# Fifteen weight tiles split afresh in every block instead of stored and read back, and splits pinned in ScalarE's order

## The chip, the cores and the metric

One core of a Trainium2 chip runs the kernel. The metric is device time in microseconds (us) of one execution. The kernel before took 2684.38 us, the median of three runs from 2678.17 to 2687.7 us.

## The reference

One inference step of a hybrid recurrent layer, all in fp32: 2048 prompt tokens and 8 x 8 sample tokens of width 1024 go through two branches (a gated linear recurrence, "LRU", and a gated delta rule with 8 heads, "GDN"), which are merged by sigmoid gates and projected.

```
u = rms_norm(x, norm_pre)                                  # [tokens, 1024]
z = u @ w_in                                               # 1024 x 8208
lru_x, lru_gate, q|k|v, gdn_gate, b, a, m_lru, m_gdn = split(z)
lru_out = rg_lru(conv4(lru_x)) * silu(lru_gate)
gdn_out = gated_delta(silu(conv4(q|k|v)), b, a) * silu(gdn_gate)
merged  = sigmoid(m_lru) * (lru_out @ w_br_lru) + sigmoid(m_gdn) * (gdn_out @ w_br_gdn)
x_new   = x + rms_norm(merged @ w_out, norm_post)
```

The columns m_lru and m_gdn of w_in are the merge gates: 16 tiles of 128 columns.

## The kernel before, in words

The prompt is worked in four blocks of 512 tokens; the 64 sample tokens ride along in block 0, so that a projection there has 576 columns, in two matmul widths of 256 and 320, and 512 columns in blocks 1 to 3. A block runs through stages: the input is normalised and transposed into eight tiles `u` (`u_norm`, `u_tile`); then the K stage (for each of 8 heads a K tile with its convolution, then a merge-gate tile), the LRU stage (8 LRU tiles, 7 more merge-gate tiles between them, 4 gate tiles), the GDN stage (Q, V and gate tile of each head, and the delta rule woven between their matmuls), the branch projections, and the output projection, into which the next block's `u` transposes are woven.

A fp32 product is made of three matmuls: a weight tile W is split into hi (rounded to the matmul's fp32r type) and lo = W - hi, the activations likewise, and a projection tile runs hi x hi, hi x lo, lo x hi for each of 8 slices of 128 rows, 24 matmuls for each width (L551, L553, L555). There are 88 weight tiles. In block 0 each is loaded raw, split (`split`: ScalarE writes hi, L143; GpSimd writes lo, L205; VectorE for the last 8), used, and stored to DRAM with both halves, 1 MB, as `dW`; in blocks 1 to 3 all 88 are read back from `dW`. `worder` lists the tiles in order of use, `wfetch` gets the next ones, `wload` issues a raw load, `wstore` the stores. In block 0 the split tiles live in a ring of three buffers `whl` and `wfetch` runs one tile ahead of the projection; later `whx` is a fourth buffer and it runs three ahead. A new split may write a buffer only when TensorE is done with the tile in it and, in block 0, when that tile's store has landed.

TensorE's order is written by the program: `Weave` decides when the other stages' generators run between a projection's matmuls. The other engines' orders, and that of the DMA issues on SyncE's queue (SP), are set by a scheduler when the program is built; every engine then runs its list strictly in order. Before, `A.after = wlast[0]` (L544) makes every ScalarE operation traced after a projection's start follow the newest weight split: the split may be placed early, but nothing newer before it. Projections write three PSUM banks (`pmm`); ScalarE or VectorE must empty a bank before TensorE can use it again. In the K stage ScalarE copies a K tile out (`cvr`, `cvy`, `cvs`), VectorE convolves it (L582, L588), ScalarE makes the tanh of it (`th`), VectorE the product `kT` (L597), TensorE the head's Gram matrix (`g<-kT`); of the merge-gate tile ScalarE makes `tmo`, at once from PSUM. `er` is the head's decay matrix: a DMA, GpSimd (L756, L757), ScalarE.

Of the kernel before, what the change touches and what calls it, by code (L numbers as in the profile page):

```python
# [22 lines left out]
F32 = mybir.dt.float32  # L23
# [42 lines left out]
LM = 7  # L66
# [88 lines left out]
def body(ctx, tc, x_prompt, x_sample, state_lru_conv, state_lru_h, state_gdn_conv, state_gdn_S,  # L155
# [84 lines left out]
    wstores, wraws = [], {}  # L240

    wready = []
    wlast = [None]
    wnext, lnext = [0], [0]
    ring, wx = [0], []

    def wtile():
        ring[0] += 1
        if wx and ring[0] % 4 == 0:
            return wx[0].tile([128, 2, 1024], F32R, name="whx", tag="whx")  # L250
        return wp.tile([128, 2, 1024], F32R, name="whl", tag="whl", bufs=3)

    def wload(n):

        src, c = e = worder[n]
        if key(e) in wraws:
            return
        if isinstance(c, tuple):
            raw = rw.tile([128, 4, 256], F32, name="rawo", tag="raws")
            SP.dma_start(raw, src[c[1] * 512:(c[1] + 1) * 512, c[0] * 256:(c[0] + 1) * 256]  # L260
                         .rearrange("(k p) c -> p k c", p=128))
            wraws[key(e)] = raw
        elif not (paired[0] <= n < paired[1] or paired[2] <= n < paired[3]):
            raw = rw.tile([128, 8, 128], F32, name="raws", tag="raws")
            SP.dma_start(raw, src[:, c:c + 128].rearrange("(k p) c -> p k c", p=128))
            wraws[key(e)] = raw
        else:
            two = [key(x) for x in worder[n:n + 7]].count((src.tensor.name, c + 128))
            w = 128 + 128 * two
            raw = rp[0].tile([128, 8, w], F32, name="raw", tag="raw")  # L270
            SP.dma_start(raw, src[:, c:c + w].rearrange("(k p) c -> p k c", p=128))
            for j in range(1 + two):
                wraws[src.tensor.name, c + 128 * j] = raw[:, :, 128 * j:128 * j + 128]
# [7 lines left out]
    def wfetch(ahead):  # L281

        while wnext[0] < len(worder) and len(wready) < ahead:
            n = wnext[0]
            e = worder[n]
            place = wplace[key(e)]
            out = isinstance(e[1], tuple)
            hl = wtile()
            hi, lo = (hl[:, j].rearrange("p (k c) -> p k c", c=256 if out else 128) for j in range(2))
            if n < len(wplace):  # L290
                while lnext[0] < len(wplace) and lnext[0] <= n + (
                        2 if paired[0] <= lnext[0] < paired[1] else 1):
                    wload(lnext[0])
                    lnext[0] += 1
                wstore(1)
                wlast[0] = split(hi, lo, wraws[key(e)], V if out else None)
                wstores.append((place, hl))
            else:
                wstore()
                SP.dma_start(hl.bitcast(F32), dW[place])  # L300
            wready.append((hi, lo))
            wnext[0] += 1
# [44 lines left out]
    def u_tile(xh, k):  # L347
        hi = pA.tile([128, TB + NS], F32R, name="a", tag="a")
        lo = pA.tile([128, TB + NS], F32R, name="a", tag="a")
        for gi, grp in enumerate([xh[:4]] + ([xh[4:]] if len(xh) > 4 else [])):  # L350
            t = gtile()
            n = 0
            for xt, m in grp:
                tr(t[:, n:n + m], xt[:m, k * 128:(k + 1) * 128], ident[:m, :m])
# [57 lines left out]
    with tc.tile_pool(name="init", bufs=2, side="right") as ip:  # L412
        with tc.tile_pool(name="u0", bufs=1) as up:
            r0 = ip.tile([8, 128], F32, name="r0")
            SP.dma_start(r0, rows(norm_pre))
            xh = u_load(0, up)
            t = gtile()
            tr(t[:, :8], r0, ident[:8, :8])
            V.tensor_copy(npre, t[:, :8])
            wraw = ip.tile([128, 8, 16], F32, name="wraw", bufs=1)  # L420
            SP.dma_start(wraw, win[:, C_B:C_B + 16].rearrange("(k p) c -> p k c", p=128))
# [8 lines left out]
            V.memset(zz, 0.0)  # L430
            V.tensor_copy(wst[:, 256:352], zz)
            V.tensor_copy(wst3[:, :, 0:16], wraw)
# [98 lines left out]
    for blkno in range(NBLK):  # L531
        if blkno == 1:
            rw_cm.__exit__(None, None, None)
            wx.append(ctx.enter_context(tc.tile_pool(name="wx", bufs=1, side="right")))
            ring[0] = 0
# [5 lines left out]
        def proj(mov, evac):  # L541
            w = nextw()
            wfetch(3 if blkno else 1)
            A.after = wlast[0]  # L544
# [808 lines left out]
```

## Time and profile before

| | |
|---|---|
| runs | 2687.7, 2678.17, 2684.38 us; median 2684.38 |
| profiled execution | 2683.59 us, span 2681.9 us |
| busy share: TensorE, VectorE, ScalarE, GpSimd | 96%, 56%, 33%, 21% |
| mean granted TensorE clock | 0.987 of full |
| DMA | 581.82 MB, mean 217 GB/s |
| blocks 0 to 3 by the stages' starts | 0 to 895, 895 to 1495, 1495 to 2094, 2094 to 2682 us |

Names in the profile are those of the program's tiles, without numbers. PE is TensorE, PEld its weight loads, DVE VectorE, ACT ScalarE, POOL GpSimd, SPq SyncE's queue of DMA issues. L143 is the helper through which all ScalarE activations are issued and L205 the subtraction in `split`, so those groups are told apart by tile: `whl<-raw` on ACT writes a hi half, `whl<-raw` on POOL a lo half. A number in brackets is how long the engine sat idle before an instruction, with what ended that wait.

### The profile page before, as it was taken

The page shows a single profiled execution, that of the slowest core. Times are in us where ns is not written, and L with a number is a line of the kernel's source. Part 1 is how long each engine was busy: PE and PEld are TensorE (multiplying, and loading weights), DVE is VectorE, ACT ScalarE, POOL GpSimd, SP SyncE. Part 2 cuts the span into 40 slices and gives each one's busy share as a digit, 9 for nine tenths or more (in the row PEclk, how much of TensorE's full clock was granted, in tenths as well). Part 3 has the DMA queues.
Part 4 walks back from the last instruction along what each step waited for, and adds up shares of the span by engine and source line. Part 5 has one row for each costly group of instructions (what it writes and reads, how often), then busy time and mean ns, then how long its engine had stood idle before and what let it go on. Part 6 is the DMA issues. An engine that isn't in the chain of part 4 may idle for free.

```text
span 2681.9 us, 39950 instructions
## 1 busy us (share of the span) xinstructions
PE 2571.7 (96%) x15332; PEld 2237.5 (83%) x15332; DVE 1503.4 (56%) x3441; ACT 885.4 (33%) x1722; POOL 565.8 (21%) x444
## 2 busy tenths in 40 slices
PE   6888799999999999999999999999999999999999
PEld 5887798888999788888889888888889888888888
DVE  4668477787434557566522557566513458566512
ACT  5324543333324225333302235333303235333301
POOL 2442342232540211100120121110210211110200
PEclk9988899999999999999999999999999999999999
DMA  7987978789887887554466787544466887555465
GB/s 190 250 257 187 228 207 187 203 176 179 255 292 256 283 277 222 200 177 158 154 237 256 260 283 225 203 163 163 154 245 256 270 272 217 200 172 168 160 236 200
DMA packets 327897, 581.82 MB, mean 217 GB/s; under 512 B 70849, under 2 KB 236762, under 8 KB 282650
## 3 DMA queue, kind: packets, MB, share of 16 engines
q1 hardware_dynamic: 313882, 553.57, 66.9%
q10 hardware_dynamic: 13824, 25.70, 2.5%
q8 instruction: 121, 1.98, 0.3%
q14 instruction: 70, 0.57, 0.1%
HBM read 421.61 MB, written 157.59 MB: 216 GB/s over the span
## 4 chain that ended last, share of the span: by engine, by line
PE 68%; DMA 3%; issue 2%; DVE 1%; POOL 1%; ACT 1%; SPq 0%; ACTq 0%; POOLq 0%; DVEq 0%
PE mm L555 17%; PE mm L551 16%; PE mm L553 16%; PE g L192 5%; PE c L192 4%; PE mm L1294 2%; PE mm L1298 2%; PE mm L1296 2%; PE g L196 2%; DMA er<-dgc 1%; DMA dgc<-gr 0%; DMA npb<-in_norm_post_dram 0%; DMA ux<-in_x_prompt_dram 0%; DMA whl<-dW 0%; POOL er L756 0%
## 5 line engine op out<-in xcount | busy, mean ns | idle before, releaser
L551 PE MATMUL mm<-a,whl 128*128 128x512 f32 (+2 forms) x2432 | 865.0, 356 | 25.2 <-ACT tmo L143 18.5
L555 PE MATMUL mm<-a,whl 128*128 128x512 f32 (+2 forms) x2432 | 869.6, 358 | 4.8 <-POOL whl L205 4.8
L553 PE MATMUL mm<-a,whl 128*128 128x512 f32 (+2 forms) x2432 | 863.9, 355 | 0.0
L551 PEld LDWEIGHTS mm<-a,whl 128*128 128x128 f32 x2432 | 466.7, 192 | 74.7 <-ACT tmo L143 20.0
L555 PEld LDWEIGHTS mm<-a,whl 128*128 128x128 f32 x2432 | 466.7, 192 | 58.0 <-POOL whl L205 5.4
L553 PEld LDWEIGHTS mm<-a,whl 128*128 128x128 f32 x2432 | 466.7, 192 | 45.6
L582 DVE SCALAR_TENSOR_TENSOR cvy<-cvr,cwg,cvy 128x512 f32<-128x512 f32 x288 | 224.7, 780 | 17.8 <-ACT cvy L143 12.4
L553 PE MATMUL mm<-a,whx 128*128 128x512 f32 x448 | 181.7, 406 | 0.0
L555 PE MATMUL mm<-a,whx 128*128 128x512 f32 x448 | 181.4, 405 | 0.0
L551 PE MATMUL mm<-a,whx 128*128 128x512 f32 x448 | 179.3, 400 | 0.0
L1232 DVE SCALAR_TENSOR_TENSOR pt<-tm,mm 128x512 f32<-128x512 f32 (+1 forms) x80 | 47.4, 592 | 189.8 <-PE mm L555 189.8
L143 ACT ACTIVATE cvr<-mm 128x512 f32<-128x512 f32 (+1 forms) x160 | 81.7, 510 | 175.4 <-PE mm L555 167.3
L1086 POOL TENSOR_TENSOR st<-st,mhalf 128x4 f32<-128x4 f32 x32 | 32.3, 1009 | 507.8 <-DVE st L1084 496.0
L205 POOL TENSOR_TENSOR whl<-raw,whl 128x1024 fp32r<-128x1024 f32 x44 | 108.8, 2474 | 118.4 <-ACT whl L143 108.6
L205 POOL TENSOR_TENSOR whl<-raws,whl 128x1024 fp32r<-128x1024 f32 x36 | 89.8, 2495 | 188.6 <-ACT whl L143 176.5
L1296 PE MATMUL mm<-whl,bt 128*128 128x256 f32 x448 | 126.4, 282 | 0.8 <-DVE whl L205 0.8
L1294 PE MATMUL mm<-whl,bt 128*128 128x256 f32 x448 | 126.2, 282 | 0.8 <-DVE y L1303 0.8
L1298 PE MATMUL mm<-whl,bt 128*128 128x256 f32 x448 | 126.2, 282 | 0.6 <-DVE yss L1272 0.6
L143 ACT ACTIVATE th<-cvy 128x512 f32<-128x512 f32 (+1 forms) x96 | 61.9, 644 | 195.7 <-DVE cvy L582 128.6
L143 ACT ACTIVATE yv<-c 128x128 f32<-128x128 f32 x128 | 35.5, 278 | 243.7 <-PE c L192 243.2
L555 PE MATMUL mm<-gp,whl 128*128 128x512 f32 (+2 forms) x296 | 104.2, 352 | 0.0
L551 PE MATMUL mm<-gp,whl 128*128 128x512 f32 (+2 forms) x296 | 104.1, 352 | 0.0
(341 smaller groups left out, 4637.8 us busy)
## 6 DMA issues: line engine op xcount, KB each, us to landing
whl<-dW SPq DMA_DIRECT2D x199, 1024.0 KB
dW<-whl SPq DMA_DIRECT2D x88, 1024.0 KB
whx<-dW SPq DMA_DIRECT2D x65, 1024.0 KB
raws<-in_w_in_dram SPq DMA_DIRECT2D x33, 512.0 KB
raw<-in_w_in_dram SPq DMA_DIRECT2D x15, 1024.0 KB
dtm<-tmo ACTq DMA_DIRECT2D x48, 256.0 KB
tm<-dtm SPq DMA_DIRECT2D x48, 256.0 KB
ux<-in_x_prompt_dram SPq DMA_DIRECT2D x16, 512.0 KB
```

The lines of the kernel that those rows point to most:

```text
L143: r = f(*args, **kw)
L192: T.matmul(out, a, b, start=start, stop=stop)
L196: T.transpose(out, in_, idn)
L205: (eng or G).tensor_tensor(out=lo, in0=src, in1=hi.bitcast(F32), op=OP.subtract)
L551: T.matmul(ps[:, :n], wh, mh[:, c0:c0 + n], start=k == 0, stop=False)
L553: T.matmul(ps[:, :n], wh, ml[:, c0:c0 + n], start=False, stop=False)
L555: T.matmul(ps[:, :n], lo[:, k, :], mh[:, c0:c0 + n], start=False, stop=k == 7)
L582: V.scalar_tensor_tensor(out=y[:, :TB], in0=raw[:, i:i + TB], scalar=cw[:, i, ti:ti + 1], in1=y[:, :TB], op0=OP.mult, op1=OP.add)
L1232: proj(mov, lambda ps, c0, n: V.scalar_tensor_tensor(out=t_[:, c0:c0 + n], in0=x[:, c0:c0 + n], scalar=1.0, in1=ps[:, :n], op0=OP.add, op1 ...
L1294: T.matmul(ps[:, :256], mh[:, cs], wh[:, k % 4], start=k == 0, stop=False)
L1296: T.matmul(ps[:, :256], mh[:, cs], wl[:, k % 4], start=False, stop=False)
L1298: T.matmul(ps[:, :256], ml[:, cs], wh[:, k % 4], start=False, stop=k == 7)
```

## The change

1. Fifteen merge-gate tiles (`whole`) are not stored in block 0. In blocks 1 to 3 they are loaded raw from w_in again, two at a time (a 1 MB pair in one new buffer `wmr`; the last one alone), and split on ScalarE and GpSimd again. `wfetch` issues the next pair's load when a tile of it is at most three ahead and none is held.
2. `A.after` is gone. In block 0 each split is pinned behind the ScalarE operation traced just before it (`tc.keep_in_program_order`). The splits of blocks 1 to 3 are not pinned.
3. The rows of w_in are dealt to partitions eight neighbours at a time (`krows`), for all raw loads of w_in. To match, `u_tile` transposes every eighth column of the input instead of 128 neighbours, so the operand that TensorE loads as weights has a step of 8 elements, 32 bytes; and `norm_pre` is loaded straight into `npre`, without a transpose.
4. Two VectorE operations of the beta/alpha weights (`zz`, the cast of `wraw` into `wst`) are pinned behind older VectorE work.

```
+    NW, NP1 = len(wplace), paired[1]
+    whole = {key(e) for e in mcol[:8 + LM]}
+    def krows(a, by8):
+        return a.rearrange("(p k) c -> p k c", k=8) if by8 else a.rearrange("(k p) c -> p k c", p=128)
...
-                wlast[0] = split(hi, lo, wraws[key(e)], V if out else None)
-                wstores.append((place, hl))
+                tc.keep_in_program_order(split(hi, lo, wraws[key(e)], V if out else None))
+                if key(e) not in whole:
+                    wstores.append((place, hl))
+            elif key(e) in whole:
+                wstore()
+                wload(n)
+                split(hi, lo, wraws.pop(key(e)))
             else:
                 wstore()
                 SP.dma_start(hl.bitcast(F32), dW[place])
+            if wx:
+                for j in range(n + 1, min(n + 4, len(worder))):
+                    if key(worder[j]) in whole:
+                        if not any(x in wraws for x in whole):
+                            wload(j)
+                        break
...
-                tr(t[:, n:n + m], xt[:m, k * 128:(k + 1) * 128], ident[:m, :m])
+                tr(t[:, n:n + m], xt[:m].rearrange("t (p k) -> t k p", k=8)[:, k], ident[:m, :m])
...
-            r0 = ip.tile([8, 128], F32, name="r0")
-            SP.dma_start(r0, rows(norm_pre))
+            SP.dma_start(npre, norm_pre.rearrange("o (p k) -> (o p) k", k=8))
...
-            V.tensor_copy(wst3[:, :, 0:16], wraw)
+            tc.keep_in_program_order(V.tensor_copy(wst3[:, :, 0:16], wraw))
...
-            A.after = wlast[0]
```

TensorE's list is the same in both programs but for the one `npre` transpose that is left out. ScalarE's list at the start of block 0, where `a<-g,npre` empties the transposed input into `u` and `whl<-raws` are the first weight splits, before:

```order
L143 ACTIVATE ux_216<-ux_216,urr 128x1024
L143 ACTIVATE whl<-raws 128x1024
L143 ACTIVATE a<-g,npre 128x512
L143 ACTIVATE a<-g,npre 128x64
L143 ACTIVATE a<-g,npre 128x512
L143 ACTIVATE whl<-raws 128x1024
L143 ACTIVATE a<-g,npre 128x64
```

and now, at the end of the same sixteen copies:

```order
L143 ACTIVATE a<-g,npre 128x512
L143 ACTIVATE a<-g,npre 128x64
L143 ACTIVATE whl<-raws 128x1024 x2
L143 ACTIVATE negA<-negA 128x8
L143 ACTIVATE zr<-mm 32x256
```

Three splits stood between the copies of `u`; now two stand behind all of them, and the third comes a tile later. ScalarE's list at one head in the middle of block 0's K stage, before:

```order
L143 ACTIVATE cvr<-mm 128x256
L143 ACTIVATE cvy<-mm,cwg 128x256
L143 ACTIVATE cvr<-mm 128x256
L143 ACTIVATE cvy<-mm,cwg 128x320
L143 ACTIVATE cvs<-mm 128x8x8
L143 ACTIVATE whl<-raw 128x1024
L143 ACTIVATE th<-cvy 128x576
L143 ACTIVATE tmo<-mm 128x256
```

and now:

```order
L143 ACTIVATE cvr<-mm 128x256
L143 ACTIVATE cvy<-mm,cwg 128x256
L143 ACTIVATE cvr<-mm 128x256
L143 ACTIVATE cvy<-mm,cwg 128x320
L143 ACTIVATE cvs<-mm 128x8x8
L143 ACTIVATE th<-cvy 128x576
L143 ACTIVATE whl<-raw 128x1024
L143 ACTIVATE tmo<-mm 128x256
```

The split has moved behind `th`, which waits for VectorE's convolution, and it is that of one tile earlier in the order of use than the split that stood there. ScalarE's list at the start of block 1's K stage, before:

```order
L143 ACTIVATE cvr<-mm 128x512
L143 ACTIVATE cvy<-mm,cwg 128x512
L143 ACTIVATE th<-cvy 128x512
L143 ACTIVATE tmo<-mm 128x512
L143 DMA dtm<-tmo 128x512
L143 ACTIVATE er<-er 128x512
```

and now, where `whl<-wmr` is the split of a merge-gate tile from its raw pair:

```order
L143 ACTIVATE cvr<-mm 128x512
L143 ACTIVATE cvy<-mm,cwg 128x512
L143 ACTIVATE th<-cvy 128x512
L143 ACTIVATE tmo<-mm 128x512
L143 ACTIVATE whl<-wmr 128x1024
L143 DMA dtm<-tmo 128x512
L143 ACTIVATE er<-er 128x512
```

One split has come in behind each merge-gate tile's `tmo`, in each of blocks 1 to 3.

## Rows read from the trace of the kernel before

**Rows 1.** The page's busy times, and the granted clock in 40 slices.

```profile
PE 2571.7 (96%) x15332; PEld 2237.5 (83%) x15332; DVE 1503.4 (56%) x3441; ACT 885.4 (33%) x1722; POOL 565.8 (21%) x444
PEclk9988899999999999999999999999999999999999
```

**Rows 2.** Busy time by stretch: window, PE, PEld, DVE, ACT, POOL, PEclk, DMA share, GB/s.

```profile
0.00:45.00 45.00, 19.76 (x86) 14.13 (x87) 14.84 (x53) 21.63 (x44) 12.58 (x21) 1.00 0.67 144
52.00:198.00 146.00, 124.69 (x863) 120.46 (x861) 93.34 (x250) 47.12 (x99) 67.75 (x48) 0.93 0.88 255
198.00:345.00 147.00, 119.29 (x801) 116.97 (x800) 102.39 (x253) 78.10 (x140) 47.26 (x29) 0.88 0.85 208
895.00:1495.00 600.00, 597.22 (x3243) 500.79 (x3242) 321.48 (x722) 187.02 (x356) 87.76 (x83) 1.00 0.64 217
```

**Rows 3.** Waits in the start, 0 to 45 us: us in total, times, longest.

```profile
PE g L196 <- DVE a L358: 10.9, 5, 5.9
ACT whl L143 <- DMA raws<-in_w_in_dram: 9.6, 3, 5.5
```

**Rows 4.** Waits in block 0's K stage, 52 to 198 us.

```profile
ACT whl L143 <- DMA dW<-whl: 29.0, 6, 8.8
PE mm L551 <- ACT tmo L143: 14.2, 4, 7.3
PE mm L555 <- POOL whl L205: 2.9, 1, 2.9
```

**Rows 5.** Waits in block 0's LRU stage, 198 to 345 us.

```profile
ACT whl L143 <- DMA dW<-whl: 18.4, 4, 8.1
ACT whl L143 <- issue: 7.0, 1, 7.0
PE g L192 <- ACT lt L143: 15.1, 2, 10.1
```

**Rows 6.** Timeline of the start: start us, us, engine, instruction, count, idle before.

```profile
31.44 1.06 ACT L143 ACTIVATE whl<-raws 128x1024 fp32r<-128x1024 f32 x1 [5.51 <-DMA raws<-in_w_in_dram]
33.92 2.75 PE L196 MATMUL g<-ident,ux 64*128 64x64 f32 x10 [5.94 <-DVE a L358]
```

**Rows 7.** Timeline of block 0, first matmuls of two tiles in a row.

```profile
51.69 0.28 PE L551 MATMUL mm<-a,whl 128*128 128x256 f32 x1
58.09 0.28 PE L551 MATMUL mm<-a,whl 128*128 128x256 f32 x1
```

**Rows 8.** Timeline of block 0's K stage, first head, fourth, and end.

```profile
52.58 0.23 ACT L143 ACTIVATE cvs<-mm 128x64 f32<-128x64 f32 x1
...
110.24 0.23 ACT L143 ACTIVATE cvs<-mm 128x64 f32<-128x64 f32 x1
...
111.50 2.77 POOL L205 TENSOR_TENSOR whl<-raw,whl 128x1024 fp32r<-128x1024 f32 x1 [2.50 <-ACT whl L143]
...
115.29 0.69 ACT L143 ACTIVATE th<-cvy 128x576 f32<-128x576 f32 x1 [3.87 <-issue]
115.88 0.69 ACT L143 ACTIVATE tmo<-mm 128x256 f32<-128x256 f32 x2
...
121.71 0.23 ACT L143 ACTIVATE cvs<-mm 128x64 f32<-128x64 f32 x1
...
124.24 0.28 DVE L588 SCALAR_TENSOR_TENSOR cvy<-cvs,cwg,cvy 128x64 f32<-128x64 f32 x1
...
198.62 0.23 ACT L143 ACTIVATE cvs<-mm 128x64 f32<-128x64 f32 x1
```

**Rows 9.** The transposes into `u`: four in a row in block 0's output projection, and all.

```profile
824.39 0.46 PEld L196 LDWEIGHTS g<-ident,ux 128*128 128x128 f32 x4
...
L196 PE MATMUL g<-ident,ux x136: 270/273/476, 7.7 to 2052.0; 128*128 128x128 f32 x128, 64*128 64x64 f32 x8
```

**Rows 10.** Timeline of block 1's K stage, one head.

```profile
962.62 0.69 DVE L597 SCALAR_TENSOR_TENSOR kT<-th,cvy 128x512 f32<-128x512 f32 x1 [0.50 <-ACT th L143]
...
963.72 1.09 PEld L192 LDWEIGHTS g<-kT 128*128 128x128 f32 x8
```

More of the change, by code (lines that the diff above doesn't have):

```diff
@@ L240, in body, with wtile @@
     wstores, wraws = [], {}
+    NW, NP1 = len(wplace), paired[1]
+    whole = {key(e) for e in mcol[:8 + LM]}
+    def krows(a, by8):
+        return a.rearrange("(p k) c -> p k c", k=8) if by8 else a.rearrange("(k p) c -> p k c", p=128)
     wready = []
-    wlast = [None]
     wnext, lnext = [0], [0]
[L245 to L249, printed above, removed]
+    wx = []
+    def wtile(n):
+        if wx and n % 4 == 0:
             return wx[0].tile([128, 2, 1024], F32R, name="whx", tag="whx")
@@ L262, in wload @@
             wraws[key(e)] = raw
-        elif not (paired[0] <= n < paired[1] or paired[2] <= n < paired[3]):
+        elif not wx and not (paired[0] <= n < paired[1] or paired[2] <= n < paired[3]):
             raw = rw.tile([128, 8, 128], F32, name="raws", tag="raws")
-            SP.dma_start(raw, src[:, c:c + 128].rearrange("(k p) c -> p k c", p=128))
+            SP.dma_start(raw, krows(src[:, c:c + 128], src is win))
             wraws[key(e)] = raw
@@ L269, in wload @@
             w = 128 + 128 * two
-            raw = rp[0].tile([128, 8, w], F32, name="raw", tag="raw")
-            SP.dma_start(raw, src[:, c:c + w].rearrange("(k p) c -> p k c", p=128))
+            raw = (wx[0].tile([128, 8, w], F32, name="wmr", tag="wmr") if wx else
+                   rp[0].tile([128, 8, w], F32, name="raw", tag="raw"))
+            SP.dma_start(raw, krows(src[:, c:c + w], src is win))
             for j in range(1 + two):
@@ L287, in wfetch @@
             out = isinstance(e[1], tuple)
-            hl = wtile()
+            hl = wtile(n)
             hi, lo = (hl[:, j].rearrange("p (k c) -> p k c", c=256 if out else 128) for j in range(2))
@@ L413, in body @@
         with tc.tile_pool(name="u0", bufs=1) as up:
-            r0 = ip.tile([8, 128], F32, name="r0")
-            SP.dma_start(r0, rows(norm_pre))
+            SP.dma_start(npre, norm_pre.rearrange("o (p k) -> (o p) k", k=8))
             xh = u_load(0, up)
-            t = gtile()
-            tr(t[:, :8], r0, ident[:8, :8])
-            V.tensor_copy(npre, t[:, :8])
             wraw = ip.tile([128, 8, 16], F32, name="wraw", bufs=1)
-            SP.dma_start(wraw, win[:, C_B:C_B + 16].rearrange("(k p) c -> p k c", p=128))
+            SP.dma_start(wraw, krows(win[:, C_B:C_B + 16], True))
             u_norm(xh, up)
@@ L429, in body @@
             zz = ip.tile([128, 96], F32, name="zz", bufs=1)
-            V.memset(zz, 0.0)
+            tc.keep_in_program_order(V.memset(zz, 0.0))
             V.tensor_copy(wst[:, 256:352], zz)
-            V.tensor_copy(wst3[:, :, 0:16], wraw)
+            tc.keep_in_program_order(V.tensor_copy(wst3[:, :, 0:16], wraw))
             V.tensor_tensor(out=wst3[:, :, 16:32], in0=wraw, in1=wst3[:, :, 0:16].bitcast(F32), op=OP.subtract)
@@ L534, in body @@
             wx.append(ctx.enter_context(tc.tile_pool(name="wx", bufs=1, side="right")))
-            ring[0] = 0
+            wraws.clear()
         sb = blkno == SB
```

## The prediction

> **What bounds the kernel now.** I read the page first, then busy time by stretch, then the waits of TensorE and ScalarE in the stretches that have gaps, and last the timelines around those gaps. On the page the reader is to see that TensorE is the busy engine, 2571.7 of 2681.9 us, and that its clock falls only in the first seventh of the run [rows 1]. The stretches say the same more sharply: block 1 is busy 597.22 of 600 us at full clock, so there is next to nothing to win in blocks 1 to 3 and something to lose; block 0 is where time lies open [rows 2]. In its K stage TensorE is idle 146 - 124.69 = 21.3 us and runs at 0.93, which costs another 0.07 x 124.69 = 8.7; in its LRU stage it is idle 27.7 and loses 0.12 x 119.29 = 14.3 to the clock; in the first 45 us it is idle 25.2 [rows 2]. Together 97 us, the stock that the change can draw on.
>
> Who ends those gaps is told by the waits. In the start TensorE waits for `a` on VectorE 10.9 us, and that waits for ScalarE, which itself sits 9.6 us in front of weight splits whose raw tiles have not landed [rows 3]; the timeline shows the last such case, ScalarE idle 5.51 us until 32.5 and TensorE idle 5.94 us right behind it [rows 6]. In the K stage ScalarE waits 29.0 us, six times, in front of a split until a store `dW<-whl` has landed and frees the buffer; TensorE's own wait is listed as `tmo`, 14.2 us, because the PSUM copy stands behind the split in ScalarE's list, and only 2.9 us are waits for a split itself [rows 4]. In the LRU stage the same wait is 18.4 us plus 7.0 without a named releaser, and TensorE's is listed as `lt`, 15.1 us [rows 5].
>
> **The start: -8 us.** Fifteen copies no longer stand behind splits that wait for DMA. Of the 10.9 us [rows 3] VectorE's own pace keeps some, since it must still make eight lo tiles; the bounds are -10.9 and 0, and I take -8. The two splits that now follow the copies cost 2 x 1.06 on ScalarE [rows 6], beside the first matmuls.
>
> **Block 0's K stage: -16 us.** Seven or eight of the 16 stores here go, so a buffer's split waits for a store only at every other tile, and that store has fewer transfers beside it. What is late next? The split that now stands behind `th`. A head now has a ring: K tile copied out (`cvs`), convolution, `th`, split, lo half, next K tile. From the fourth head: `cvs` to `th` 115.29 - 110.24 = 5.05, `th` to the next ScalarE operation 0.59, hi 1.06, lo 2.77 [rows 6, 8]: 9.5 us. TensorE needs lo at its third matmul and then runs the rest of the 6.40 us tile [rows 7], some 6.2, and the copies take about 1 more (an estimate, from three short copies): 16.7 us a head. In the fifth head the convolution ended 124.52 - 121.71 = 2.8 us behind `cvs` [rows 8], which makes it about 14.8. TensorE's own work is 2 x 6.40 plus the 863 - 768 matmuls that belong to no projection, 95 x 6.40/48 / 8 = 1.6, so 14.4. Before, a head took (198.62 - 52.58)/8 = 18.3 [rows 8]. The middle of 14.8 and 16.7 is 15.8, which is 2.5 less, 20 us over eight heads. I take 4 off, because the first heads lose a split that had been done one tile ahead, and their `th` is later than the others'. Bounds: all of 21.3 + 8.7 = -30; and +10, if every head takes 1.3 us more than before, in a ring in which VectorE is held up as well.
>
> **Block 0's LRU stage: -14 us.** Here the split stands behind the copies, not behind `th`, so the ring above does not form. ScalarE's 18.4 + 7.0 us in front of splits [rows 5] should mostly go, with half of the stores gone. Not all of TensorE's 27.7 + 14.3 = 42 us hangs on it: part is gate arithmetic on a busy VectorE (102.39 of 147 us [rows 2]). I take a third, and bounds of -30 and 0.
>
> **The rest of block 0: 0 us.** In the GDN stage the pinned splits have more TensorE work between two projections to hide behind; the branch and output weights are handled as before. No wait of these stages is touched by name, so the bounds are narrow estimates, -4 and +5.
>
> **The transposes: +8 us.** Each of the 136 now loads its weights with a step of 32 bytes. Four of them in a row took 0.46 us of weight loading, 0.107 apart [rows 9], so nothing hides a slower load there. The 40 of block 0 lie in the start, at VectorE's pace; 96 lie in full output projections. No row shows such a load. The nearest row is the load as it was, which gives 0; from the other side, a transpose that gets no overlap at all takes 272 instead of 107 ns [rows 9], 96 x 0.165 = 16 us. I take the middle, because the same number of columns speaks for the one end and a pattern that no instruction here uses for the other. The bound below nothing is excluded: nothing is left out of the load.
> The Trainium skill, SBUF — State Buffer, Door 1: The DMA port swizzle, notes that SBUF lines are 16 bytes and that each access to a new line pays, fp32 being free only up to a step of four. No run here shows it yet. Were each load twice as long by it, the term would be an estimated 96 x 0.107 = 10 us and the sum 2 us more.
>
> **Splits in blocks 1 to 3: +9 us.** Each block gets 15 more ScalarE and GpSimd operations, 1.06 and some 2.4 to 2.8 us [rows 6, 8]: 16 us on an engine busy 187 of 600 and 40 on one busy 88 [rows 2]. The split of a tile can begin when TensorE is done with the tile four before, three tiles ahead of its use, against some 4 us of split: hidden. Queued behind the ScalarE split are `er` and the next K tile's copies, behind the GpSimd one the next head's `er`; the raw load waits on SP for the pair buffer, with the reads of `dW` and `er` behind it. The slack is thin where it is paid: `kT` ended at 963.31 and its Gram load began at 963.72, 0.4 us later [rows 10]. I take 3 us a block: 15 splits, of which one in five pushes TensorE by one ScalarE split of 1.06. Bounds: 0 (fewer bytes read might even help, but TensorE is full, so not below 0), and 30, if two thirds of 45 splits push it by 1.
>
> **Sum.** 2683.59 - 8 - 16 - 14 + 8 + 9 = 2662.6. The profiled execution lies 0.8 us under the median of the runs shown: 2663 us.
>
> **Rivals.**
> *The pinned split takes the place of the store.* TensorE now waits for `POOL whl` in every head of the K stage, as long as it waited for `tmo`, and the gaps keep the clock down. For it: the ring of 16.7 us is above TensorE's 14.4 even without a late DMA. Against: it is below 18.3. The K stage gives 0, the LRU stage half, -7: 2683.6 - 8 - 7 + 8 + 5 = 2682.
> *Slower, through blocks 1 to 3.* GpSimd's lo half holds up the K stage of every full block: it stands in front of `er` or beside the convolution, and each head then pays what exceeds the slack, 2.4 - 0.4 = 2 us. For it: 0.4 us of slack, and in block 0 a convolution took 5.05 us with a split beside it and 2.8 without [rows 8, 10]. Against: the split comes behind `tmo`, a tile away from the next convolution. Price 24 heads x 2 = 48 in place of 9: 2663 + 39 = 2702. It decides from about 1.8 us a head on, where it passes 2663 + 30.
> *The change doesn't do what it says*, that is, the store waits stay because the remaining stores land no sooner: ScalarE's 29.0 and 18.4 remain; start -8, transposes and splits +17: 2692.
> *All of it at once*: both stages run free and transposes cost nothing: -8 - 24 - 24 + 4, 2632.
>
> **How the numbers follow.** What a measurement of this kernel can tell from no change is about 0.3%, 8 us. Chances: forecast 0.50 (its own range 2652 to 2674), all at once 0.09, the pinned split in the store's place 0.20, slower through blocks 1 to 3 0.14, stores no sooner 0.07. Faster by over 0.3%: the forecast and the best case, rounded to 0.60. Within: the pinned split, 0.20. Slower: the last two, rounded to 0.20. The sum of all outer bounds is 2620 to 2738; for eight times in ten the range stops at 2638, short of the best case, and at 2696, which takes in two rivals and leaves out most of the slow one.
>
> **What would show it.** Right: no ScalarE `whl` waits for `raws` before 30 us and the matmul that stood at 51.69 us [rows 7] some 7 us earlier; in the K stage `whl<-dW` waits under 10 us, `cvs` of successive heads 15 to 16.5 us apart and some 1 to 2 us a head of TensorE waiting for `POOL whl`; clock of the two stages above 0.95; block 1 still 600 us or a little over, its gaps in the K stage; the four transposes 0.107 to 0.27 apart. Wrong: heads still 18 us apart; a full block of over 610 us; or block 0 no shorter than 885 us.

## The result: 2789.5 us, 4% slower

The changed kernel takes 2789.54 us (2788.4 to 2790.62, four runs), the kernel before 2683.2 on the same chip (2678.17 to 2687.7, four runs): a ratio of 1.0397, 95% interval 1.0377 to 1.0416. The prediction was 2663, its range 2638 to 2696; both the sign and the size were wrong.

The profile after, first the page's lines that answer to [rows 1], columns as there:

```profile
PE 2609.3 (94%) x15331; PEld 2262.3 (81%) x15331; DVE 1508.2 (54%) x3440; ACT 929.7 (33%) x1767; POOL 663.6 (24%) x489
PEclk9999999999999999999999989999999999999999
```

TensorE is busy 37.6 us longer with the same matmuls, at a mean granted clock of 0.972 in place of 0.987, and idle the rest of the 105.5 us by which the span grew. Next the stretches that answer to [rows 2]: the start, block 0's K stage and LRU stage at their new places, and block 1 from its first `kT` to that of block 2.

```profile
0.00:45.00 45.00, 27.52 (x142) 21.83 (x143) 21.83 (x76) 27.43 (x58) 10.31 (x20) 1.00 0.80 151
45.00:188.00 143.00, 117.26 (x803) 112.48 (x802) 78.83 (x237) 45.14 (x92) 60.73 (x45) 0.90 0.83 218
188.00:330.00 142.00, 124.23 (x862) 121.95 (x860) 112.52 (x266) 80.64 (x145) 53.94 (x32) 0.93 0.67 161
906.00:1536.00 630.00, 607.23 (x3241) 506.97 (x3240) 334.03 (x720) 200.93 (x371) 122.89 (x98) 0.98 0.62 194
```

Block 1 holds TensorE's same matmuls in 630 us in place of 600: 22.8 us idle, and 10 us more busy at a mean granted clock of 0.98.

How the two kernels drift apart is best read from one instruction that each block has. The first `kT` of blocks 0 to 3 starts at 60.04, 895.90, 1495.34 and 2093.53 us before, and at 50.36, 906.44, 1536.54 and 2167.03 after; the spans are 2681.9 and 2787.4. So the start won 9.7. Block 0's last `kT` is at 190.05 before and 184.25 after, 5.8 ahead: the K stage gave back 3.9. Over all VectorE, ScalarE and GpSimd instructions that both traces hold, the median lead is 20.3 between 420 and 500 us, so the LRU stage and the start of the GDN stage won 14.5. From there block 0 loses 30.8, and the three later blocks lose 30.7, 32.3 and 32.0. The sum: -9.7 + 3.9 - 14.5 + 30.8 + 95.0 = 105.5. Where one stage ends and the next begins is a choice, and the first three terms hang on it. By the copies `cvs` that the prediction used [rows 8], the K stage runs from 52.58 to 198.62 us before and from 45.06 to 203.71 after: the start won 7.5, the K stage lost 12.6, and the LRU stage won 25.4, with the same sum of 20.3.

**Block 0.** The waits that answer to [rows 3 to 5]: TensorE's longest in the start, then ScalarE's, GpSimd's and TensorE's in the K stage, then TensorE's in the LRU stage.

```profile
PE g L196 <- DVE uss L357: 8.0, 1, 8.0
...
ACT er L143 <- POOL er L769: 26.2, 7, 6.8
...
ACT whl L143 <- POOL whl L205: 2.9, 2, 2.2
POOL er L768 <- DMA er<-dgc: 20.9, 5, 7.6
...
PE mm L567 <- POOL whl L205: 22.8, 9, 7.8
...
PE mm L563 <- ACT tmo L143: 7.7, 2, 4.0
PE g L192 <- ACT xh L143: 5.6, 1, 5.6
PE mm L567 <- POOL whl L205: 5.0, 5, 1.8
```

The 29.0 and 18.4 us in which ScalarE waited in front of a split for a store are gone but for 1.9 us, as intended. In the K stage TensorE now waits 22.8 us for GpSimd's half of the split, more than the 14.2 + 2.9 it lost before. What makes GpSimd's half late in the third head is `er`, which stands before it in GpSimd's list and whose load comes late: ScalarE's half starts at 89.15 us and GpSimd's only at 96.21, behind two `er`, the first of which had waited 5.32 us for its load.

**The K stage of blocks 1 to 3**, where 76 of the 95 us go: from a block's first `kT` to its last it takes 114.2, 115.1 and 115.1 us, before 89.8, 89.0 and 89.5. The rest of each block is 6 to 7 us longer. In block 2's K stage TensorE is busy 95.61 us at a granted clock of 0.92, before 88.37 at 1.00; the other 19.6 us are idle, before 0.6. Block 2, one head whose raw pair is being loaded, on SP's queue, ScalarE, GpSimd, VectorE and TensorE (start us, us, engine, instruction, idle before and what ended it), and after the dots the next head:

```profile
1589.87 0.55 SPq L276 DMA_DIRECT2D wmr<-in_w_in_dram  x1
1590.51 0.61 SPq L311 DMA_DIRECT2D whx<-dW  x1
1594.28 2.85 SPq L766 DMA_DIRECT2D er<-dgc  x1
1604.19 1.06 ACT L143 ACTIVATE whl<-wmr 128x1024 fp32r<-128x1024 f32 x1 [6.97 <-DMA wmr<-in_w_in_dram]
1610.73 1.04 POOL L768 TENSOR_TENSOR er<-er,gcs 128x512 f32<-128x512 f32 x1 [19.31 <-DMA er<-dgc]
1611.73 2.39 POOL L205 TENSOR_TENSOR whl<-wmr,whl 128x1024 fp32r<-128x1024 f32 x1
1614.74 0.63 ACT L143 ACTIVATE er<-er 128x512 f32<-128x512 f32 x1 [9.49 <-POOL er L769]
1615.78 0.60 ACT L143 ACTIVATE cvr<-mm 128x512 f32<-128x512 f32 x1 [0.40 <-ACT er L143]
1621.02 0.69 DVE L609 SCALAR_TENSOR_TENSOR kT<-th,cvy 128x512 f32<-128x512 f32 x1 [0.49 <-ACT th L143]
1621.77 2.07 PE L192 MATMUL g<-kT 128*128 128x128 f32 x8 [6.51 <-DVE kT L609]
...
1622.38 1.04 POOL L768 TENSOR_TENSOR er<-er,gcs 128x512 f32<-128x512 f32 x1 [6.69 <-DVE kT L609]
1623.38 2.38 POOL L205 TENSOR_TENSOR whl<-wmr,whl 128x1024 fp32r<-128x1024 f32 x1
1626.39 0.63 ACT L143 ACTIVATE er<-er 128x512 f32<-128x512 f32 x1 [3.97 <-POOL er L769]
1632.68 0.69 DVE L609 SCALAR_TENSOR_TENSOR kT<-th,cvy 128x512 f32<-128x512 f32 x1 [0.50 <-ACT th L143]
```

Read it upwards from TensorE. The Gram product waits 6.51 us for `kT`; `kT` is late because ScalarE copied the K tile out of PSUM only at 1615.78; the copy stands in ScalarE's list behind `er`, which waits for GpSimd's `er`; and that waited 19.31 us until the load `er<-dgc` had landed. This load was issued at 1594.28, behind the raw pair and a stored tile. In the next head no pair is on its way: the split stands at the same place and takes the same 2.38 us, and `kT` follows 11.66 us behind the last; before, the same two heads stood 12.0 apart. The split alone does no harm here; the head with a load takes 24.3, before 11.5. From issue to GpSimd's use, the `er` loads of blocks 1 to 3 take 4.3 to 8.3 us before, and 11.1 to 16.5 in six heads after, two in each block.

The load is slow, not large. Busy share of the 16 DMA engines and GB/s in 40 slices, first of the kernel before from 1500 to 1590 us, then of the changed one from 1532 to 1660 (3.2 us a slice):

```profile
DMA  9793697796989994299999999788999638997899
GB/s 324 175 395 119 109 372 333 273 339 203 132 320 374 410 360 163 66 273 371 426 372 183 192 398 427 313 182 139 370 391 379 196 130 359 374 374 253 221 389 275
```

```profile
DMA  9951745899999955643999997026429899613429
GB/s 169 299 218 22 311 131 198 90 93 77 165 407 320 256 231 186 166 152 49 86 95 83 365 394 316 10 82 154 174 28 158 174 400 391 246 45 104 138 82 136
```

With stored tiles, 8 KB in a row for each partition, the best slices move 370 to 427 GB/s; others with busy engines move less, where smaller transfers mix in. In slices 20 to 22 after, the three behind 1592.8 us, the engines are just as busy and move 83 to 95: that is the raw pair, read from `w_in` in pieces of 1 KB. It takes 14.3 us from issue to the split. By the DMA records of the trace, the pair's 1,024 pieces run from 1591.2 to 1603.9 us: a third of them take 44 to 47 ns, the mean is 179 ns, and the slowest tenth takes over 382. At 46 ns a piece, sixteen engines would move an estimated 16 x 1,024 B / 46 ns = 356 GB/s. So a piece of 1 KB is not slow in itself; most pieces of this load are held up, and by what is not shown.

**The GDN stage of block 0**, where 16 of the 30.8 us go (the lead falls from 20.3 to 4.4 by 700 us of the kernel before). Before, ScalarE's and GpSimd's splits of one stretch; after, the same two engines, TensorE behind them, and that wait of TensorE from 420 to 720 us in total:

```profile
547.21 1.08 ACT L143 ACTIVATE whl<-raws 128x1024 fp32r<-128x1024 f32 x1
548.37 2.51 POOL L205 TENSOR_TENSOR whl<-raws,whl 128x1024 fp32r<-128x1024 f32 x1 [8.98 <-ACT whl L143]
553.96 1.06 ACT L143 ACTIVATE whl<-raws 128x1024 fp32r<-128x1024 f32 x1
555.09 2.39 POOL L205 TENSOR_TENSOR whl<-raws,whl 128x1024 fp32r<-128x1024 f32 x1 [1.24 <-ACT whl L143]
```

```profile
537.18 0.69 ACT L143 ACTIVATE th<-cvy 128x576 f32<-128x576 f32 x1 [2.02 <-DVE st L1096]
537.77 1.04 ACT L143 ACTIVATE whl<-raws 128x1024 fp32r<-128x1024 f32 x1
539.44 1.05 ACT L143 ACTIVATE whl<-raws 128x1024 fp32r<-128x1024 f32 x1
538.89 5.30 POOL L205 TENSOR_TENSOR whl<-raws,whl 128x1024 fp32r<-128x1024 f32 x2 [0.64 <-ACT whl L143]
541.90 0.39 PE L567 MATMUL mm<-a,whl 128*128 128x256 f32 x1 [2.52 <-POOL whl L205]
...
PE mm L567 <- POOL whl L205: 17.2, 7, 2.5
```

Pinned, two of a head's three splits come together behind `th`, which waits for VectorE; the first has lost the 6.8 us that it was ahead, and TensorE waits 2.52 us for its lo half, once in a head, seven times. The other 14.8 us go in the branch and output projections: from 720 to 910 us TensorE waits 4.9 us for VectorE's lo halves, 2.3 for ScalarE's hi halves and 2.0 for a last lo half of GpSimd, in place of 0.8, 0 and 0, at a granted clock of 0.97 in place of 1.00 (720 to 895 us).

### The profile page after: what moved, and what is told of

Its sections match the earlier page's. It is cut to its first block, busy times and chain, and to the rows that moved or that the text cites. A ratio compares the mean times of both kernels' runs of the same rounds, so it can differ in the third digit from the quotient of the medians.

```text
span 2787.4 us, 40012 instructions
## 1 busy us (share of the span) xinstructions
PE 2609.3 (94%) x15331; PEld 2262.3 (81%) x15331; DVE 1508.2 (54%) x3440; ACT 929.7 (33%) x1767; POOL 663.6 (24%) x489
## 5 line engine op out<-in xcount | busy, mean ns | idle before, releaser
L594 DVE SCALAR_TENSOR_TENSOR cvy<-cvr,cwg,cvy 128x512 f32<-128x512 f32 x288 | 215.9, 750 | 18.4 <-ACT cvy L143 13.0
L567 PE MATMUL mm<-a,whx 128*128 128x512 f32 x448 | 186.3, 416 | 0.0
L563 PE MATMUL mm<-a,whx 128*128 128x512 f32 x448 | 182.3, 407 | 3.3 <-DMA whx<-dW 3.3
L565 PE MATMUL mm<-a,whx 128*128 128x512 f32 x448 | 184.2, 411 | 0.0
L1098 POOL TENSOR_TENSOR st<-st,mhalf 128x4 f32<-128x4 f32 x32 | 32.3, 1008 | 553.4 <-DVE st L1096 503.0
L205 POOL TENSOR_TENSOR whl<-wmr,whl 128x1024 fp32r<-128x1024 f32 x45 | 111.9, 2486 | 214.8 <-ACT whl L143 209.3
L143 ACT ACTIVATE bt<-pt 128x512 fp32r<-128x512 f32 (+1 forms) x32 | 20.6, 644 | 279.4 <-POOL pt L1254 273.5
```

The costliest lines, as they stand in the source:

```text
L143: r = f(*args, **kw)
L205: (eng or G).tensor_tensor(out=lo, in0=src, in1=hi.bitcast(F32), op=OP.subtract)
L563: T.matmul(ps[:, :n], wh, mh[:, c0:c0 + n], start=k == 0, stop=False)
L565: T.matmul(ps[:, :n], wh, ml[:, c0:c0 + n], start=False, stop=False)
L567: T.matmul(ps[:, :n], lo[:, k, :], mh[:, c0:c0 + n], start=False, stop=k == 7)
L594: V.scalar_tensor_tensor(out=y[:, :TB], in0=raw[:, i:i + TB], scalar=cw[:, i, ti:ti + 1], in1=y[:, :TB], op0=OP.mult, op1=OP.add)
```

## The experiments

Two theories stood at the start. *The reload*: blocks 1 to 3 lose by the fifteen tiles split afresh, either by their loads or by the splits' work. *The pins or the rows*: the new places of the splits, or the strided transposes, make the loss. All times are medians; the kernel before, run beside each group on the same chip, had medians of 2678.8 to 2683.2. "Block 0" is the start of block 1's first `kT`, "block 1" the time to that of block 2, both from the profile:

| run | us | ratio, 95% interval | block 0 | block 1 |
|---|---|---|---|---|
| before | 2683.2 | | 895.9 | 599.4 |
| the change | 2789.5 | 1.0377 to 1.0416 | 906.4 | 630.1 |
| e1 no reload | 2707.0 | 1.0083 to 1.0121 | 910.5 | 602.5 |
| e2 reload only | 2750.1 | 1.0242 to 1.0284 | 858.7 | 632.8 |
| e3 two buffers | 2775.3 | 1.0338 to 1.0381 | 905.1 | 626.7 |
| e4 no pins | 2738.9 | 1.0202 to 1.0244 | 855.4 | 630.7 |
| e6 long rows | 2661.5 | 0.9909 to 0.9954 | 858.1 | 603.5 |
| e7 ScalarE's queue | 2731.4 | 1.0170 to 1.0218 | 860.6 | 632.7 |
| e8 splits, one load | 2649.8 | 0.9864 to 0.9914 | 853.5 | 601.5 |
| e9 rows only | 2665.6 | 0.9934 to 0.9961 | 874.3 | 602.7 |
| e13 pins only | 2718.0 | 1.0134 to 1.0170 | 923.1 | 602.8 |
| e15 pins, K and LRU | 2685.9 | 1.0008 to 1.0034 | 896.1 | 603.6 |
| e10 early copies | 2690.2 | 1.0024 to 1.0053 | 888.4 | 601.7 |
| e11 late copies | 2689.4 | 1.0024 to 1.0050 | 886.7 | 603.7 |
| e12 the same, two buffers | 2689.2 | 1.0021 to 1.0046 | 887.6 | 603.4 |
| e14 LRU stage's tiles | 2686.9 | 1.0015 to 1.0039 | 869.6 | 610.2 |
| e16 K stage's tiles | 2684.5 | 1.0005 to 1.0031 | 860.1 | 614.9 |
| e18 the same, two buffers | 2671.0 | 0.9953 to 0.9978 | 856.8 | 609.0 |
| e17 K stage's tiles, copied | 2656.7 | 0.9905 to 0.9934 | 867.8 | 597.5 |

**Which part.** One edit each undoes or does one part of the change:

```diff
# e1, the changed kernel
-    whole = {key(e) for e in mcol[:8 + LM]}
+    whole = set()
# e4, the changed kernel
-                tc.keep_in_program_order(split(hi, lo, wraws[key(e)], V if out else None))
+                wlast[0] = split(hi, lo, wraws[key(e)], V if out else None)
...
+            A.after = wlast[0]
# e2: as e4, and by8, the strided transposes and the npre load undone
# e9: as e4, and whole = set();  e13: the kernel before with the pins alone
```

> The set of tiles that are split afresh is empty: all 88 tiles are stored in block 0 and read back in blocks 1 to 3, as before the change; the pinned splits, the dealt rows and the strided transposes stay. The theory that the reload makes the loss: the three later blocks, 631 us each in the changed kernel, go back to about 600, and the time to about 2789 - 95 = 2695, up to 2715 if block 0 loses what its fewer stores had given. The rival that pins or row layout make the loss: the later blocks stay near 630, the time at 2780 or more.

> The kernel before with only the reload of fifteen tiles added: no pins, splits before every projection as before, rows and transposes as before. If the reload makes the loss: the three later blocks near 631 us, the time between 2755 and 2785. If the layout or the pins make it: 2670 to 2695, later blocks near 600.

> The changed kernel with the splits of block 0 not pinned but traced as the order before had them (before each projection, behind the last traced ScalarE operation), reload and row layout kept. If the pins cost block 0's GDN stage its 16 us: that stage falls from 41.4 to about 38.5 us a head, but the K stage may lose some of the 20 us it won; time 2770 to 2795, later blocks unchanged at 631. If the pins are what the start and the K stage gained from: 2800 to 2815.

> The kernel before with only the dealt rows of w_in, the strided transposes and the direct load of the norm weights: no pins, all 88 tiles stored. The prediction's term for the transposes, +8, would give 2685 to 2695. The two runs with the reload and no pins, 2750 without and 2739 with these rows, speak for no loss or a gain of some 11: 2665 to 2683.

> The kernel before with only the pinned splits and casts: no reload, rows as before. Theory that the pins alone are a loss, a TensorE that waits for GpSimd's half of the split in block 0: with rows at nothing this is the run of pins and rows, 2700 to 2715, and block 0 some 14 us longer. The prediction's own view, in which the pins take the splits out of ScalarE's way: 2660 to 2675.

The reload by itself costs 70 us by the medians (63 by the profiled runs): it wins 37 in block 0 and loses 33 to 34 in each later block. The pins by themselves cost 38 (31 by the profiled runs, 27 of them in block 0, 923.1 against 895.9). The rows by themselves win 14. The later blocks follow the reload alone, and that theory holds; but the pins are a second loss: taking them out wins 51 us, where e4's expectation had at most 20. And the parts do not add up: -14 + 70 + 38 is 94, the whole is 106. Without pins the missing stores bring block 0 from 874.3 to 855.4, 19 us; with pins from 910.5 to 906.4, 4 us. A likely reason, not tested: a splitter that waits for `th` anyway has no use for a buffer that comes free sooner. The times of e2 and e13 lie 5 and 3 us outside the ranges of the theories that they support.

**Why the reload costs.** A ring of one buffer, the splits' work, or the load itself:

```diff
# e3, the changed kernel
-            raw = (wx[0].tile([128, 8, w], F32, name="wmr", tag="wmr") if wx else
+            raw = (wx[0].tile([128, 8, w], F32, name="wmr", tag="wmr", bufs=2) if wx else
# e6, on e4, in blocks 1 to 3
-            SP.dma_start(raw, krows(src[:, c:c + w], src is win))
+            SP.dma_start(raw.rearrange("p k c -> p (k c)"),
+                         dW[wplace[key(worder[n - 1])]].rearrange("p j c -> p (j c)")[:, :8 * w])
# e7, on e4 with two buffers
+            (A if wx else SP).dma_start(raw, krows(src[:, c:c + w], src is win))
# e8, on e4: one load, every split reads it
+                if not kept:
+                    kept.append(wx[0].tile([128, 8, 256], F32, name="wmr", tag="wmr"))
+                    SP.dma_start(kept[0], krows(src[:, c:c + w], src is win))
+                raw = kept[0]
```

> The changed kernel with two buffers for the reloaded raw pairs in place of one. Theory of the ring: the loss is the wait for a pair whose load can only be issued when the last split of the pair before has ended, so a second buffer takes most of the 95 us away: 2700 to 2725, later blocks 600 to 608, no ScalarE split that waits for a raw pair. Rival, the work itself: the splits stand in front of the er operations and the convolution's copies whenever they come, and the later blocks stay at 620 to 631 us, the time at 2760 to 2790.

> The kernel without pins (2739 us) in which blocks 1 to 3 read each raw pair's 1 MB from a stored tile, 8 KB in a row for each partition, in place of 1 KB pieces of w_in; the values of these fifteen tiles are then others. Theory of the slow load: in the profiles the queue moves 80 to 160 GB/s while a raw pair is read and 370 to 420 with stored tiles, and the er load issued behind it lands some 7 us late in every second head; with long rows the load takes some 3 us, and most of the 32 us a block goes: 2645 to 2670. Rival, the single buffer and the place of the load: 1 MB is still issued late, a split still waits: 2715 to 2740. Rival, the splits' own work: 2730 to 2740.

> The kernel without pins with two raw buffers, and the raw pair's load issued by ScalarE on its own queue, so that the er load does not stand behind it on SP's. If the order within SP's queue makes er late: blocks 1 to 3 near 605 to 610 us, time 2655 to 2685. If the 16 DMA engines are simply held by the slow load, whichever queue issued it: as the second buffer gave, 4 to 5 us a block, 2715 to 2730.

> The kernel without pins in which the raw pair is loaded once and every later split of blocks 1 to 3 takes its values from that buffer: all 45 splits, one load. If the loads make the loss: blocks 1 to 3 at 600 to 606 us, time 2640 to 2660, with 0.3 us a head left for the splits. If the splits' own work, 1.06 us on ScalarE and 2.4 us on GpSimd in front of the er operations, makes it: blocks 625 to 632, 2715 to 2740.

The second buffer takes only 3 to 6 us a block: the ring was the first theory, and it falls. With all 45 splits and one load (e8) the block is at 601.5, so the splits' work is nearly free; with the same bytes in long rows, from other tiles (e6), it is at 603.5. The way the pair is read, in 1 KB pieces of `w_in`, is the price: 77 of the 89 us between e4 and e8 go with it. Another queue and a second buffer together (e7) change little: block 1 is as long as in e4, blocks 2 and 3 are 6 and 5 us shorter, about what the second buffer alone gave in e3. `er` is late there too, 9.6 to 10.9 us from issue to use in the same six heads, though no pair stands before it on SP's queue; so the load holds the DMA engines and not only SP's list. TensorE's waits in block 2's K and LRU stages, the changed kernel (1536 to 1720 us), then e6 (1461 to 1640), then e8 (1455 to 1640):

```profile
PE g L192 <- DVE kT L609: 18.0, 3, 7.1
PE mm L563 <- DMA whx<-dW: 2.3, 1, 2.3
```

```profile
PE g L192 <- ACT xh L143: 2.0, 2, 1.6
PE g L192 <- DVE kT L615: 1.6, 2, 1.3
```

```profile
PE g L192 <- ACT xh L143: 1.8, 2, 1.6
PE g L192 <- DVE xl L205: 0.5, 2, 0.2
```

The wait for `kT` goes from 18.0 to 1.6 to none.

**Where the pins cost.** e15 pins in block 0's K and LRU stages alone (`if n < paired[1]`), and traces the splits of the GDN stage as before:

> The kernel before with the splits pinned only in block 0's K and LRU stages and traced as before from the GDN stage on. In the run with all pins block 0 was 6 us ahead at 420 us and 25 behind at 880, with two splits in a row behind each head's th in the GDN stage. If that is where pins lose: 2670 to 2682. If they lose through the order of later blocks: 2700 to 2712.

It came out at 2685.9, 4 us above its range, 32 us below all pins and 7 above none: the loss is that of the GDN stage and what follows it. TensorE's waits from 420 to 720 us in e15 no longer hold a wait for a split:

```profile
PE g L196 <- DVE cvy L619: 9.4, 7, 1.3
PE c L192 <- DVE S L1094: 6.8, 7, 1.3
```

while with all pins (e13) the pair behind `th` stands there as in the changed kernel:

```profile
553.24 5.29 POOL L205 TENSOR_TENSOR whl<-raws,whl 128x1024 fp32r<-128x1024 f32 x2 [0.64 <-ACT whl L143]
...
556.26 0.58 PE L571 MATMUL mm<-a,whl 128*128 128x256 f32 x1 [2.54 <-POOL whl L205]
```

**Where the loads cost.** The set cut to the LRU stage's seven tiles or the K stage's eight, on e4 (`mcol[8:8 + LM]`, `mcol[:8]`):

> The kernel without pins that splits afresh only the seven merge-gate tiles of the LRU stage; the eight of the K stage are stored and read back. If the raw loads cost what they cost because the er load of the K stage lands late behind them: blocks 1 to 3 lose 3 to 6 us each here, block 0 keeps the 20 us of the rows and most of what the LRU stage won, and the time is 2650 to 2668, faster than both kernels. If a raw load costs 2 us of TensorE wherever it stands: seven of fifteen loads, 15 us a block: 2680 to 2700.

> The complement: only the eight tiles of the K stage are split afresh. If the late er load is the price: 23 to 28 us a block in blocks 1 to 3, and less of block 0's 40 us: 2730 to 2750. If every raw load costs the same: 16 us a block, 2690 to 2715.

The theory of the late `er` does not hold alone: blocks 1 to 3 lose 11, 9 and 8 us with the LRU stage's seven tiles and 15, 15 and 9 with the K stage's eight, near the rival in which a load costs the same anywhere; e16's time lies below both of its ranges. Nor do the two sets add up to all fifteen: the K stage of a block loses 6 to 15 us with its own eight tiles, and 25 to 27 with all (e4). The late `er` is the way the loss takes in the K stage. With the LRU stage's tiles 6 to 7 us are lost behind the last `kT`; in block 2 TensorE waits 3.3 us there for `xh`, the LRU tile that ScalarE writes, which it does not before.

**Can the stores' gain be kept?** In e10 and e11 block 0 copies the raw columns once, memory to memory, into 8 KB rows:

```diff
+                if rcopy and n >= paired[1] and n % 3 == 0:
+                    tc.keep_in_program_order(SP.dma_start(*rcopy.pop(0)))     # e10: not held in place
...
+            SP.dma_start(raw, dR[key(e)] if wx else krows(src[:, c:c + w], src is win))
```

> The kernel without pins in which block 0's GDN stage copies the raw columns of the fifteen tiles once, memory to memory, into 8 KB rows, which blocks 1 to 3 then read. Theory of the slow load: blocks 1 to 3 as with long rows; block 0 keeps its 40 us but for what the copies take from the DMA engines, 0 to 10 us: 2645 to 2680, faster than both kernels if below 2670. Rival, splits or the single buffer: 2715 to 2745.

> The kernel without pins, with the memory-to-memory copies of the fifteen raw tiles held at their places in block 0's GDN stage, one in every third projection; in the run before they had all been issued from 200 to 330 us, where block 0 fell back by 30 us. Theory of the slow load: the 30 us come back but for some 2 to 10 us that the copies take in the new place: 2655 to 2672, faster than both kernels. If the copies cost the same wherever they lie: 2685 to 2695.

> The same with two buffers for the raw pairs, so that a load is issued before the last split of the pair before. If the single buffer is what is left of the reload's cost, 4 us a block: 2645 to 2662. If what is left is the splits' own work: as with one buffer, 2655 to 2672.

The later blocks are cured with real data (602 to 604, with one buffer or two), but the copies are themselves read in 1 KB pieces and cost block 0 its gain, so that all three runs miss the range that was hoped for. In e10 the copies are issued from 140 to 328 us, in the K and LRU stages. In e11 they are held at their places from 321 to 589 us. Its lead over before is 32 us behind the first three, where e4, without copies, goes on to 41. The rest goes in one single wait:

```profile
471.90 2.48 PE L192 MATMUL g<-Sall,dia 128*128 128x128 f32 x10 [22.22 <-DMA Sall<-in_state_gdn_S_dram]
```

Behind the copy issued at 427.0 the next raw load is issued at 446.1 and takes 9.47 us to issue; the load of the sample tokens' states, `Sall`, comes only at 458.6, and TensorE waits 22.2 us for it (21.0 in e12). The lead falls from 32.1 to 8.0 there and stays at 8.0 while four more copies are issued, at 479 to 589 us. So e11 lost not by a price for each copy, as e17's expectation has it, but by one late load. The last step takes four copies before that place (`n % 2`), and the K stage's tiles alone; beside it stands the other way, short pieces issued earlier:

> The kernel without pins that splits only the K stage's eight tiles afresh, and reads their four raw pairs in blocks 1 to 3 from copies in 8 KB rows; the four copies are issued at every other projection from the start of block 0's GDN stage on, where the run with eight copies lost 3 us for the first three of them. Block 0 should be 30 to 35 us shorter than before, and blocks 1 to 3 lose some 8/15 of the 18 us that fifteen tiles in long rows lost: 2652 to 2668, faster than both kernels and than the rows alone (2666) if the copies cost under 4 us. If the copies cost 6 us each, as the later ones of the run with eight did: 2672 to 2685.

> The same eight tiles with raw loads in 1 KB pieces as in the change, and two raw buffers. The second buffer took 4 to 5 us a block from fifteen tiles' cost of 32; from eight tiles' 13 it should take 2 to 5: 2670 to 2680.

e17 takes 2656.7 us, faster than before by 0.8% (0.66 to 0.95) and than the change by 133 us; its block 1 is at 597.5. The rows alone (e9) are faster by 0.5%, so keeping the stores' gain adds some 0.3%. That e17's time lies in its range is in part luck: block 0 gained 28 us and not 30 to 35, and the later blocks lost nothing where some 10 us in all were expected. e18 gets half of the way from e16 to e17. The page of e17, with TensorE busy 13 us less than before:

```profile
PE 2558.5 (96%) x15331; PEld 2227.7 (84%) x15331; DVE 1518.6 (57%) x3440; ACT 907.7 (34%) x1746; POOL 624.3 (24%) x468
```

## Why the prediction was wrong

*The step that failed* is "Splits in blocks 1 to 3: +9 us", with bounds of 0 and 30. It measured +95. The split it priced rightly: e8 has 2.0, 2.4 and 4.9 us for it in blocks 1 to 3, 9 in all. It named the raw load on SP "with the reads of `dW` and `er` behind it" and then gave it nothing, because fewer bytes are read. Its price was in sight, in the trace of before: block 0 reads raw pairs in the same pieces. Busy share and GB/s there from 80 to 144 us (1.6 us a slice; a pair is issued at 109.01):

```profile
DMA  9899997517998968999989999999999999999979
GB/s 376 215 129 123 228 247 183 182 68 237 355 427 356 364 192 272 409 387 320 206 82 119 106 165 134 103 263 440 403 346 271 86 132 251 323 343 385 344 263 394
```

Slices 21 to 26, from 112 to 122 us, show 82 to 165 GB/s on busy engines. At 82 the three or four pairs of a K stage are 1.05 MB / 82 GB/s = 12.8 us each, and not the 2.7 of a stored tile at 394. The pair shown in block 2 took 12.6 us from its first piece to the end of its last. The bound of 30 was built from the split's time, and so left out the term that decided. The Trainium skill, DMA: Bandwidth & Descriptors, Specifications, gives 512 B as the least transfer for full line rate; by it alone the 1 KB pieces would cost no more than long rows, which the third of them that took 44 to 47 ns agree with, and the load as a whole, at 179 ns in the mean, does not. Perfetto Trace Analysis, DMA Optimizations, of the Trainium skill says that transfers under 2 KB carry much overhead and that 4 or 8 KB move far more; e6 agrees in direction, with 27 us less in block 1. Whether the cause is the length of the pieces, where they start (rows of `w_in` are 32,832 bytes apart) or the order in which they are read was not tried; the fast third speaks against the length alone.

*The rest of block 0: 0 us*, bounds -4 and +5, measured +30.8; e13 and e15 give it to the pins. "More TensorE work between two projections to hide behind" looked at the spacing of projections, and not at what the pinned split now stands behind: `th`, which waits for VectorE, so that two of three splits come in a pair; and "handled as before" left out that the pins hold the branch and output weights' splits too, where the other half of the loss lies.

*Block 0's K stage: -16* came to +3.9 by `kT`, and to +12.6 by the prediction's own rows. The ring was seen, with `th`, split, lo half and next tile, but it is longer: `cvs` of successive heads stood 16.5 to 24.1 us apart, 19.8 in the mean, against the 15 to 16.5 expected and 18.3 before, and TensorE waited nine times, 2.5 us in the mean and 7.8 at most, for GpSimd. What the ring left out is at least `er` in GpSimd's list, with 20.9 us of waiting for its loads; how the 4 us a head between 15.8 and 19.8 divide was not taken apart. The rival "the pinned split takes the place of the store" is what happened in this stage, with 22.8 us in place of 17.1.

*The start: -8* measured -9.7 by `kT` and -7.5 by `cvs`: right, and for the reason given; ScalarE waits for no raw tile before 30 us, and the matmul that stood at 51.69 us stands at 44.17. *The LRU stage: -14* measured -14.5 by the one mark and -25.4 by the other: the direction is right, and the waits for stores are gone as it said, but that a third of 42 us fits so well is luck of the mark. Nor were the pins a help to the K and LRU stages: without them (e4) the median lead between 420 and 500 us is 41.2 in place of 20.3.

*The transposes: +8* were too dear. The loads of [rows 9] after:

```profile
841.76 0.53 PEld L196 LDWEIGHTS g<-ident,ux 128*128 128x128 f32 x4
...
L196 PEld LDWEIGHTS g<-ident,ux x136: 182/193/230, 7.9 to 2125.4; 128*128 128x128 f32 x128, 64*128 64x128 f32 x8
```

A load takes 193 ns at the median, four overlapped ones 0.53 us in place of 0.46: 96 x 0.07 / 4 = 1.7 us in all. The Trainium skill, SBUF — State Buffer, Door 1, says that each new line of 16 bytes costs; that agrees, with 193 ns against the 141 that the trace of before has for the same load. Most of the longer load is overlapped, as the 0.53 us show. That the rows as a whole win 14 us was not foreseen at all. e9 has it in block 0, where its K stage (52 to 198 us) moves 273 GB/s against 255, and a 1 KB piece takes 91 ns in the mean against 109; whether by the new order of the rows in the raw loads or by the rest of that edit was not taken apart.

*The slower rival* had the right place, the K stage of every full block, and chance 0.14; its mechanism, GpSimd's lo half, is refuted by e8, and its 48 us were half of what came. One part of the loss is in no step for blocks 1 to 3: of block 1's 30.7 us, 10 are the same matmuls at a lower granted clock, 0.98 over the block at levels of 1.2 and 2.4 GHz. In block 2 the lower clock lies in the K stage with its gaps, 0.92 there and 0.99 behind.

In the working itself four numbers slipped, and none decides: ScalarE's wait [rows 6] ended at 31.44 us and not at 32.5, where the split ended; 16.7 less 5.05 plus 2.8 is 14.5 us and not 14.8; the slow rival passes 2663 + 30 from 1.6 us a head on, not 1.8; and the outer bounds add up to 2609 to 2745, not 2620 to 2738. The measured time lies outside of these too. All three signs of being wrong came: heads 19.8 us apart, a full block of 630 us, and block 0 at 906.

## What to carry to other kernels

Price a transfer by its way of reading and not by its bytes: read the GB/s of the same access pattern where the trace already has it, and ask which small load stands behind it. A work item that is pinned behind a waiting instruction inherits that wait; see what stood between the two before. When a change has several parts, measure them singly first: here one part won 14 us, one lost 38 and one lost 70, and the winner could not be seen in the sum.

## What the runs showed of the hardware

Sixteen DMA engines, busy over 90%, moved 83 to 95 GB/s while a raw pair was read from `w_in` in 1 KB pieces (44 to 47 ns for a third of the pieces, 179 ns in the mean), and 370 to 427 GB/s in the best slices with 8 KB rows. Memory-to-memory copies of 1 MB of the same columns had no fixed price: behind one, issued at 427.0 us in e11, TensorE waited 22.2 us for a late load, and four issued at 479 to 589 us left its lead at 8.0. Raw loads issued by ScalarE in place of SP, with two buffers, left block 1 as long as it was, 632.7 against 630.7. A weight load of 128x128 with a step of 32 bytes took 193 ns at the median, without a step 141.
